# Norm gains moved from the weight rows to the transposed activations, on one core of a two-layer hybrid block

## The chip, the cores and the metric
The kernel runs on one core of a Trainium2 chip. The metric is the device time of one execution in microseconds, median of three runs. TensorE is PE in the profile, VectorE DVE, ScalarE ACT, GpSimd POOL, and SP is the engine whose queue issues the loads.

## The reference, cut to what matters
Batch 1, 256 tokens, width 1024, two layers. Each layer is an FFN, a mixer and a second FFN, each behind an rms norm with a gain vector of 1024 entries:
```
for l in range(DEPTH):
    x = x + 0.5 * swiglu(rms_norm(x, norm_ffn1[l]), ffn1_wi[l], ffn1_wo[l])
    h = rms_norm(x, norm_mix[l])
    (u, q_raw, k_cmp, ..., gate_a, gate_b) = jnp.split(h @ w_in[l], SPLIT_POINTS, axis=-1)
    y_a = s5_branch(u, ...);  y_b = nsa_branch(q_raw, ...) @ nsa_w_up[l]
    x = x + (sigmoid(gate_a) * y_a + sigmoid(gate_b) * y_b) @ w_out[l]
    x = x + 0.5 * swiglu(rms_norm(x, norm_ffn2[l]), ffn2_wi[l], ffn2_wo[l])
# rms_norm(x, g) = x * rsqrt(mean(x*x) + eps) * g
```
The S5 branch is a state space scan over 32 groups. The attention branch has compressed, selected and window keys. D_FF is 2816 and w_in has 3864 columns.

## The kernel before
All weights pass once through a stream of chunks of 128 rows by up to 1024 columns (plan, line 195; most hold two k tiles of 512 columns, those of the third and second mixer products two of 408 and two of 384). A chunk is loaded into a `raw` buffer by the SP queue (`load`, `_dma`) and then split into two numbers of the product's type, `whi` (the rounded value) and `wlo` (the rest), ScalarE writing the one and VectorE the other (`_split0`). A product is three matmuls (`mm3`, lines 350 to 352): hi with hi, hi with lo, lo with hi. There are four buffers each of `raw`, `whi` and `wlo`, and `next` prepares two chunks ahead of the one in use.

The norm's factor 1/rms is a number for each token and is applied after the product, when PSUM is read. Its gain is a number for each row of the weight: where a product follows a norm (the first product of both FFNs and all of w_in), `add` notes which gain vector and which k tile a chunk has, and `_split0` multiplies the rows while it splits them, one k tile at a time (lines 154 to 158): a scaled ACTIVATE on ScalarE and a SCALAR_TENSOR_TENSOR on VectorE for each half. The gains stand as columns in `gcol`, made by a transpose at the start (`gain_cols`, line 290). Chunks without gains (the second product of an FFN, the up-projections, w_out) are split whole by `split` (line 318), as one CAST and one TENSOR_TENSOR.

The activations come token-major in `x`. `transp4` (line 340) transposes 128 tokens by 512 channels on TensorE into one PSUM bank and splits them into `hh` and `hl` with one instruction on each engine. It runs four times at the start and four times in `finish` (line 354), at each of the five boundaries between phases; tile 0's two calls go between the last products of the phase, tile 1's between the first ones of the next. `finish` also leaves a fence: the next chunk's split is queued behind the first subtraction of tile 1. `transp4` serves the merged branches too (line 1293), where there is no norm.

Inside the first FFN of each layer a background generator (`prep`, line 1328) issues the preparation of the S5 branch a little at a time: elementwise work on VectorE and POOL, and transposes on TensorE (line 761). In the mixer another one (`s5_main`, `attn_units`) issues the scan and the attention between the weight products. There line 822 copies a rearranged input on POOL (profiled as line 480), `compress` (line 1020) makes the compressed keys from four chunks that are not split (lines 230 to 233) and then runs its GELU on ScalarE (`hid`, line 1040), and the gates' tanh is line 1264. In the FFN line 451 is the gated product on VectorE, and line 434 its transposes.

The order of instructions on every engine is set by a planner at build time, which goes by program order and by its own prices of instructions; SP's loads keep program order, and `issue_after` puts an instruction behind another on its engine. The functions that the change touches:

Of the kernel before, what the change touches and what calls it, by code (L numbers as in the profile page):

```python
# [7 lines left out]
F32 = mybir.dt.float32  # L8
F32R = mybir.dt.float32r
BF = mybir.dt.bfloat16  # L10
AF = mybir.ActivationFunctionType
ALU = mybir.AluOpType
# [5 lines left out]
L = 2  # L18
# [6 lines left out]
# column offsets of the shape-only constants, packed side by side on 128 partitions  # L25
# [49 lines left out]
class Model:  # L75
# [31 lines left out]
    def add(k, ap, split=True, g=None):  # L107
        """g: (norm, first k tile) whose gains scale the rows"""
        k.chunks.append((ap, split, g))
# [31 lines left out]
    def _split0(k, i):  # L141
        r = k.raw.pop(i)
        if not k.chunks[i][1]:
            k.hl[i] = r
            return
        hi = k.pw.tile([128, 1024], F32R, name="whi", bufs=k.opt['nh'])
        lo = k.pw.tile([128, 1024], F32R, name="wlo", bufs=k.opt['nh'])
        g = k.chunks[i][2]
        if g is None:
            k.split(r, hi, lo)  # L150
        else:
            sh = [n for _, n in k.chunks[i][0].ap[1:]]
            kt, w = sh[0], int(np.prod(sh[1:]))
            for j in range(kt):
                s, c = slice(j * w, (j + 1) * w), k.gcol[:, g[0] * 8 + g[1] + j:g[0] * 8 + g[1] + j + 1]
                k.hi_ins[i] = k.nc.scalar.activation(hi[:, s], r[:, s], AF.Copy, scale=c)  # L156
                k.nc.vector.scalar_tensor_tensor(lo[:, s], r[:, s], c, hi[:, s].bitcast(F32), op0=ALU.mult,  # L157
                                                 op1=ALU.subtract)
        k.hl[i] = (hi, lo)
# [15 lines left out]
    def next(k, la=None):  # L175
        """the next chunk of the stream; prepares later ones as far as buffers allow"""
        i = k.nu
        k.nu += 1
        if i and not k.chunks[i - 1][1]:
            k.held -= 1  # L180
        k.prepare(k.opt['LA'] if la is None else la)
        k.pull()
        return k.hl.pop(i)
# [11 lines left out]
    def plan(k):  # L195
# [13 lines left out]
        def ffn(l, wi, wo, n):  # L209
            for c in range(NFF):  # L210
                for i in range(4):
                    k.add(ap2(wi, l, i * 256, 2, c * 256, DFF, 256), g=(n * 2 + l, i * 2))
                for i in range(2):
                    if c:
                        k.add(ap(wo, l, (c - 1) * 256 + i * 128, 1, 0, D))
            for i in range(2):
                k.add(ap(wo, l, (NFF - 1) * 256 + i * 128, 1, 0, D))

        def cols(l, c0, n=512):
            for i in range(4):  # L220
                k.add(ap(k.a['w_in'], l, i * 256, 2, c0, n), g=(2 + l, i * 2))

        A = k.a
        for l in range(L):
            ffn(l, A['ffn1_wi'], A['ffn1_wo'], 0)
            cols(l, C_U)
            cols(l, C_KC, 384)
            cols(l, C_VS, 408)
            w1 = A['cmp_w1']
            for kv in range(2):  # L230
                for i in range(2):
                    k.add(bass.AP(tensor=w1.tensor, offset=w1.offset + ((l * 2 + kv) * 2048 + i * 1024) * 128,
                                  ap=[[128, 128], [128 * 128, 8], [1, 128]]), split=False)
            for c0 in (C_Q, C_GA, C_GA + 512, C_GB, C_GB + 512):
                cols(l, c0)
            for c in range(4):
                for i in range(2):
                    k.add(ap2(A['ssm_w_glu'], l, i * 256, 2, c * 256, D, 256))
            for c in range(2):
                for i in range(2):  # L240
                    w = A['nsa_w_up']
                    k.add(tuple(bass.AP(tensor=w.tensor, offset=w.offset + (l * 512 + g * 256 + i * 128) * D + c * 512,
                                        ap=[[D, 64], [64 * D, 2], [1, 512]]) for g in range(2)))
            for i in range(8):
                k.add(ap(A['w_out'], l, i * 128, 1, 0, D))
            ffn(l, A['ffn2_wi'], A['ffn2_wo'], 2)

# [6 lines left out]
    def setup(k):  # L254
# [42 lines left out]
        for h in range(2):  # L297
            for t in range(2):
                f = k.transp4(k.x[:, t, h * 512:(h + 1) * 512], t, h)
# [16 lines left out]
    def split(k, src, hi, lo):  # L316
        """hi: src rounded to the product's type, lo: the rest"""
        return k.nc.scalar.copy(hi, src), k.nc.vector.tensor_sub(lo, src, hi.bitcast(F32))  # L318

    def rsqrt(k, ss, n, scale):  # L320
        """(ss*scale + eps)^-0.5 on [P, n]"""
# [13 lines left out]
    def norms(k):  # L335
        """1/rms of both token tiles, behind the weight preparation issued so far"""
        with k.tc.issue_after(k.hi_ins[k.ns - k.opt['SQ']].ins):
            k.rn = [k.rstd(t) for t in range(2)]

    def transp4(k, src, t, half):  # L340
        """four 128x128 transposes of token-major src [128, 512] into hh/hl"""
# [4 lines left out]
        return k.split(b, k.hh[:, s, q], k.hl_[:, s, q]) + (m,)  # L346
# [7 lines left out]
    def finish(k, ys, sc, norm, parts):  # L354
        """x += sc * y and its transposed copy for the next phase. parts: the last products of token tile 0,
        and those of token tile 1 in two portions"""
# [7 lines left out]
        def tr(t):  # L364
            return [k.transp4(k.x[:, t, h * 512:(h + 1) * 512], t, h) for h in range(2)]
# [15 lines left out]
    def gemm(k, stat, nk, cols, order=None, per=2, la=None):  # L381
        """two token tiles against the next weight chunks; returns the two banks.
        order: chunks per turn of a tile where the turns are to be kept"""
# [33 lines left out]
    def ffn(k, hooks, sc, norm, order):  # L417
# [60 lines left out]
        k.finish(y, sc, norm, (lambda: part(0, 0), lambda: wo_mm(last - 1, 1, 1, W), lambda: part(1, 0)))  # L478
# [3 lines left out]
    def mm_cols(k, out, pairs, first, last=True):  # L482
        """sum of lhsT.T @ rhs over pairs, as two column tiles of the array that run side by side"""
# [8 lines left out]
    def s5_load(k, l):  # L492
        """DMAs of the S5 parameters of layer l"""
# [30 lines left out]
    def cmul(k, o, a, b, tmp, cost, M=None, conj=False):  # L524
        """(o0 + i o1) = (a0 +- i a1)(b0 + i b1), products on engine M; tmp(): scratch"""
# [18 lines left out]
    def s5_scalars(k):  # L544
# [31 lines left out]
        # angle to [-pi, pi]  # L576
# [19 lines left out]
        # expm1(a) = 2t/(1-t), cos-1 = -2 sin^2(th/2)  # L596
# [62 lines left out]
        # mag^4 and the unit rotation to the fourth power  # L659
# [11 lines left out]
    def s5_tables(k):  # L671
        """cos, sin of j*phi [128, 16, 64] and the decay of the scan"""
# [46 lines left out]
    def s5_mats(k):  # L719
# [7 lines left out]
        # powers times Bbar, dense: X[(g2 n), p, tau, c], tau = 3 - power  # L727
# [5 lines left out]
        # C transposed, pair-diagonal: CT[(g2 n), p, (g2' c)]  # L733
# [14 lines left out]
        # pair-diagonal copies, then the end-of-chunk input matrices  # L748
# [16 lines left out]
        # lag matrices: rows (tau, g2', c') hold lag 3 - tau  # L765
# [32 lines left out]
        # state-to-output matrices with abar^(s+1)  # L798
# [8 lines left out]
    def s5_main(k, uT):  # L807
        """uT [128 channels, 4, 256] -> yT hi/lo [128 channels, 4, 256]"""
# [56 lines left out]
    def rotate(k, out, x, cs, sn, sl, sign):  # L865
        """out = x * exp(-i*sign*phi*j); for sign < 0 the result is shifted to the next chunk"""
# [40 lines left out]
    def nsa_prep(k, l):  # L907
# [5 lines left out]
        # gains folded into the rotation; 0: q (with the score scale), 1: selection k, 2: window k  # L913
# [23 lines left out]
    def normrope(k, src, nh, cg, sg, out, tabs):  # L937
        """per-head rms norm and rope: src [P, nh, 64] (PSUM) -> out; cg/sg broadcast to [P, nh, 64]"""
# [20 lines left out]
    def kv_evac(k, t, kp, ps):  # L959
        """kp: keys before the norm [128 tokens, 2 branches, 2 heads, 64], ps [tokens, vs | kw | vw | gates]"""  # L960
# [59 lines left out]
    def compress(k, kvT):  # L1020
        """kvT [128 (h d), kv, 256 tokens] -> compressed keys and values"""
# [19 lines left out]
        # keys  # L1041
# [9 lines left out]
    def compress2(k, hid, kb):  # L1051
# [6 lines left out]
        # values  # L1058
# [9 lines left out]
    def u_cmp(k, t):  # L1068
        """compressed branch of query tile t as three stages"""
# [23 lines left out]
        def b():  # L1093
# [5 lines left out]
            # heads come as (r, g), gates as (g, r)  # L1099
# [19 lines left out]
    def u_attn(k, t, r):  # L1119
        """selection and window branches of head r of both groups for query tile t"""  # L1120
# [66 lines left out]
    def attn_units(k):  # L1187
        """the units of both query tiles, three stages deep"""
# [15 lines left out]
    def mix(k):  # L1204
# [107 lines left out]
        k.finish(y, 0.25, True, (lambda: part(0, 0, 3), lambda: part(1, 0, 1), lambda: part(1, 1, 3)))  # L1312
# [6 lines left out]
    def run(k):  # L1319
# [3 lines left out]
        for l in range(L):  # L1323
# [18 lines left out]
            k.ffn({6: h_nsa, 8: lambda: k.nsa_prep(l)}, 0.5, True, k.turns(k.opt['O2'] if l else k.opt['O1']))  # L1342
            k.drain_bg()
            k.mix()
            k.ffn({}, 0.5, l + 1 < L, k.turns(k.opt['O2']))
# [29 lines left out]
```

## Time and profile before

| what | value |
|---|---|
| median of three runs | 1202.55 us (1201.87 to 1202.59) |
| span of the profiled execution | 1202.1 us |
| TensorE busy | 1162.6 us, 97% |
| VectorE busy | 844.5 us, 70% |
| ScalarE busy | 687.7 us, 57% |
| POOL busy | 251.4 us, 21% |
| TensorE's granted clock, mean | 0.995 |

The span runs from the first to the last instruction of one profiled execution; its own time beyond that is not listed. Busy time is the sum over instructions, where matmuls overlap. A row with xN holds N instructions that follow each other, its second number their time together. The bracket behind a row is the engine's idle time just before, and what ended it.

### The profile page before, as it was taken

What the parts mean: (1) busy time and instruction counts of PE and PEld (TensorE: products, weight loads), DVE (VectorE), ACT (ScalarE), POOL (GpSimd) and SP (SyncE); (2) the same over time, 40 slices, a digit from 0 to 9 for tenths busy, and PEclk for the clock granted to TensorE, in tenths of its full rate; (3) what the DMA queues carried; (4) which work ended last, traced back from release to release, by engine and by line L of the source; (5) the groups of instructions that cost most, each with busy time, mean ns of one, the idle gap of its engine ahead of it and who ended that gap; (6) DMA issues with size and microseconds to landing.
All of it is one profiled execution on the core that took longest, in us unless ns stands there. A gap on an engine that the chain in (4) does not pass through costs nothing. (4 is left out here: it accounts for less than half of the span.)

```text
span 1202.1 us, 18057 instructions
## 1 busy us (share of the span) xinstructions
PE 1162.6 (97%) x6326; PEld 947.3 (79%) x6326; DVE 844.5 (70%) x1466; ACT 687.7 (57%) x1228; POOL 251.4 (21%) x320
## 2 busy tenths in 40 slices
PE   7999999989999999999999999999899999999998
PEld 6888777877777888888888887778677778888886
DVE  5797979686865765555667987986967765655554
ACT  6655554738855565555566555555597645655552
POOL 3002654273212000000020053815532110000000
PEclk9999999999999999999999999999899999999999
DMA  7766555453543566656666656455635535666662
GB/s 234 220 182 186 166 156 183 116 158 112 178 126 98 175 210 185 186 182 187 189 183 183 196 160 181 140 155 147 193 89 158 132 117 172 210 179 189 192 183 80
DMA packets 150076, 200.44 MB, mean 167 GB/s; under 512 B 9952, under 2 KB 120832, under 8 KB 149984
## 3 DMA queue, kind: packets, MB, share of 16 engines
q1 hardware_dynamic: 148848, 197.46, 54.0%
q0 software_dynamic: 1136, 1.82, 0.9%
q8 instruction: 50, 0.82, 0.3%
q14 instruction: 42, 0.34, 0.1%
HBM read 198.18 MB, written 1.05 MB: 166 GB/s over the span
## 5 line engine op out<-in xcount | busy, mean ns | idle before, releaser
L157 DVE SCALAR_TENSOR_TENSOR wlo<-raw,gcol,whi 128x512 fp32r<-128x512 f32 (+2 forms) x480 | 363.6, 797 | 104.8 <-ACT whi L156 102.3
L156 ACT ACTIVATE whi<-raw,gcol 128x512 fp32r<-128x512 f32 (+2 forms) x480 | 315.0, 710 | 174.4 <-PE gu L351 78.0
L350 PE MATMUL gu<-whi,hh 128*128 128x512 f32 (+2 forms) x960 | 380.9, 397 | 13.0 <-ACT whi L156 10.6
L352 PE MATMUL gu<-wlo,hh 128*128 128x512 f32 (+2 forms) x960 | 376.1, 395 | 0.0
L351 PE MATMUL gu<-whi,hl 128*128 128x512 f32 (+2 forms) x960 | 375.9, 392 | 0.0
L318 DVE TENSOR_TENSOR wlo<-raw,whi 128x1024 fp32r<-128x1024 f32 x128 | 162.7, 1276 | 109.3 <-ACT whi L318 104.5
L350 PEld LDWEIGHTS gu<-whi,hh 128*128 128x128 f32 x960 | 181.9, 189 | 48.5 <-ACT whi L156 10.8
L318 ACT CAST whi<-raw 128x1024 fp32r<-128x1024 f32 x128 | 134.6, 1054 | 138.2 <-PE gu L351 123.0
L351 PEld LDWEIGHTS gu<-whi,hl 128*128 128x128 f32 x960 | 181.9, 190 | 35.7
L352 PEld LDWEIGHTS gu<-wlo,hh 128*128 128x128 f32 x960 | 181.5, 189 | 35.7 <-DVE wlo L157 0.2
L325 POOL TENSOR_SCALAR rs<-ss 128x1 f32<-128x1 f32 (+3 forms) x22 | 6.6, 301 | 388.7 <-ACT w2k L332 356.0
L351 PE MATMUL yb<-whi,w1k 128*128 128x512 f32 x176 | 71.5, 406 | 0.7 <-DVE w1k L318 0.7
L352 PE MATMUL yb<-wlo,w1k 128*128 128x512 f32 x176 | 69.1, 393 | 0.0
L350 PE MATMUL yb<-whi,w1k 128*128 128x512 f32 x176 | 69.0, 395 | 0.0
L351 PE MATMUL ya<-whi,w1k 128*128 128x512 f32 x176 | 68.8, 391 | 0.0
L352 PE MATMUL ya<-wlo,w1k 128*128 128x512 f32 x176 | 68.7, 390 | 0.0
L350 PE MATMUL ya<-whi,w1k 128*128 128x512 f32 x176 | 68.2, 393 | 0.0
L318 ACT CAST w1k<-tr 128x256 fp32r<-128x256 f32 x88 | 32.4, 369 | 46.3 <-PE tr L434 46.2
L1159 POOL TENSOR_SCALAR w2k<-w2k,sm 128x128 f32<-128x128 f32 (+1 forms) x64 | 33.8, 546 | 109.3 <-ACT w2k L1143 92.4
L451 DVE SCALAR_TENSOR_TENSOR w1k<-gu,rs,w1k 128x256 f32<-128x256 f32 x88 | 41.9, 478 | 20.1 <-ACT w1k L450 20.1
L450 ACT ACTIVATE w1k<-gu,rs 128x256 f32<-128x256 f32 x88 | 40.8, 466 | 21.7 <-PE gu L352 16.8
L318 DVE TENSOR_TENSOR w1k<-tr,w1k 128x256 fp32r<-128x256 f32 x88 | 36.7, 418 | 10.4 <-ACT w1k L318 10.3
(307 smaller groups left out, 1511.2 us busy)
## 6 DMA issues: line engine op xcount, KB each, us to landing
raw<-in_ffn_wi_dram SPq DMA_DIRECT2D x352, 256.0 KB, 3.3
raw<-in_ffn_wo_dram SPq DMA_DIRECT2D x88, 512.0 KB, 3.7
raw<-in_w_in_dram SPq DMA_DIRECT2D x48, 512.0 KB, 4.5
raw<-in_ssm_w_glu_dram SPq DMA_DIRECT2D x32, 256.0 KB, 3.3
raw<-in_w_out_dram SPq DMA_DIRECT2D x16, 512.0 KB, 3.9
raw<-in_cmp_w_dram SPq DMA_DIRECT2D x8, 512.0 KB, 5.5
raw<-in_nsa_w_up_dram SPq DMA_DIRECT2D x16, 256.0 KB, 4.2
raw<-in_w_in_dram SPq DMA_DIRECT2D x8, 408.0 KB, 4.1
```

The lines of the kernel that those rows point to most:

```text
L156: k.hi_ins[i] = k.nc.scalar.activation(hi[:, s], r[:, s], AF.Copy, scale=c)
L157: k.nc.vector.scalar_tensor_tensor(lo[:, s], r[:, s], c, hi[:, s].bitcast(F32), op0=ALU.mult, op1=ALU.subtract)
L318: return k.nc.scalar.copy(hi, src), k.nc.vector.tensor_sub(lo, src, hi.bitcast(F32))
L325: k.nc.gpsimd.tensor_scalar(a, ss, scale, EPS, op0=ALU.mult, op1=ALU.add)
L350: mm(ps, a[0], b[0], start=first, stop=False)
L351: mm(ps, a[1], b[0], start=False, stop=False)
L352: return mm(ps, a[0], b[1], start=False, stop=last)
L450: m = nc.scalar.activation(sg, ps[t][:, :256], AF.Silu, scale=r[t])
L451: nc.vector.scalar_tensor_tensor(a, ps[t][:, 256:], r[t], sg, op0=ALU.mult, op1=ALU.mult)
L1159: G.tensor_scalar(w[:, i], p[:, i], cf[:, j:j + 1], 0.0, op0=ALU.mult, op1=ALU.add)
```

## The change
The gains are no longer multiplied into the weight rows. `add` forgets them, and every chunk that is split goes through `split` in one piece over its whole width (1024 columns, 816 or 768 in the two narrower products of w_in). In their place `transp4` gets the number `g` of the gain vector whose norm follows, and then splits each of its four 128x128 tiles by itself, with that k tile's gain column as the scale on ScalarE and as the factor on VectorE. `finish` hands `g` down: ffn1 gives the mixer's vector (2 + l), the mixer gives ffn2's (4 + l), ffn2 the next layer's ffn1 (l + 1) or None at the end; the first calls have 0. The call on the merged branches has no `g` and stays as it was.
```diff
 def _split0(k, i):
     ...
-    g = k.chunks[i][2]
-    if g is None:
-        k.split(r, hi, lo)
-    else:
-        sh = [n for _, n in k.chunks[i][0].ap[1:]]
-        kt, w = sh[0], int(np.prod(sh[1:]))
-        for j in range(kt):
-            s, c = slice(j * w, (j + 1) * w), k.gcol[:, g[0] * 8 + g[1] + j:g[0] * 8 + g[1] + j + 1]
-            k.hi_ins[i] = k.nc.scalar.activation(hi[:, s], r[:, s], AF.Copy, scale=c)
-            k.nc.vector.scalar_tensor_tensor(lo[:, s], r[:, s], c, hi[:, s].bitcast(F32), op0=ALU.mult,
-                                             op1=ALU.subtract)
+    sh = [n for _, n in k.chunks[i][0].ap[1:]] if not isinstance(k.chunks[i][0], tuple) else [1024]
+    n = int(np.prod(sh))
+    k.hi_ins[i] = k.split(r[:, :n], hi[:, :n], lo[:, :n])[0]
     k.hl[i] = (hi, lo)
...
-def transp4(k, src, t, half):
+def transp4(k, src, t, half, g=None):
     b = k.bank((128, 4, 128))
     for i in range(4):
         m = k.nc.tensor.transpose(b[:, i], src[:, i * 128:(i + 1) * 128], k.id)
     s, q = slice(half * 4, half * 4 + 4), slice(t * 128, (t + 1) * 128)
-    return k.split(b, k.hh[:, s, q], k.hl_[:, s, q]) + (m,)
+    if g is None:
+        return k.split(b, k.hh[:, s, q], k.hl_[:, s, q]) + (m,)
+    for i in range(4):
+        j = half * 4 + i
+        c, hi = k.gcol[:, g * 8 + j:g * 8 + j + 1], k.hh[:, j, q]
+        f = k.nc.scalar.activation(hi, b[:, i], AF.Copy, scale=c)
+        d = k.nc.vector.scalar_tensor_tensor(k.hl_[:, j, q], b[:, i], c, hi.bitcast(F32), op0=ALU.mult,
+                                             op1=ALU.subtract)
+    return f, d, m
```

## Rows read from the trace of the kernel before
**Rows 1.** The page's busy times: us, share of the span, instructions.
```profile
PE 1162.6 (97%) x6326; PEld 947.3 (79%) x6326; DVE 844.5 (70%) x1466; ACT 687.7 (57%) x1228; POOL 251.4 (21%) x320
```
**Rows 2.** Groups by form: busy us, mean ns of one, idle before and releasers.
```profile
L157 DVE SCALAR_TENSOR_TENSOR wlo<-raw,gcol,whi 128x512 fp32r<-128x512 f32 x448 | 342.4, 803 | 97.9 <-ACT whi L156 95.4 <-PE yb L352 1.5
L156 ACT ACTIVATE whi<-raw,gcol 128x512 fp32r<-128x512 f32 x448 | 297.2, 716 | 171.5 <-PE gu L351 75.6 <-PE yb L351 74.4 <-DMA raw<-in_ffn_wi_dram 8.3
...
L318 DVE TENSOR_TENSOR wlo<-raw,whi 128x1024 fp32r<-128x1024 f32 x128 | 162.7, 1276 | 109.3 <-ACT whi L318 104.5 <-PE tr L1169 3.9
L318 ACT CAST whi<-raw 128x1024 fp32r<-128x1024 f32 x128 | 134.6, 1054 | 138.2 <-PE gu L351 123.0 <-DMA raw<-in_ffn_wo_dram 11.5 <-PE yb L351 1.9
```
**Rows 3.** TensorE's waits: us in total, times, longest us.
```profile
PE gu L350 <- ACT whi L156: 10.6, 2, 5.3
...
PE tr L761 <- DVE w1k L318: 2.8, 2, 1.4
PE tr L434 <- DVE w1k L451: 2.6, 2, 1.3
PE gu L350 <- ACT r L1264: 2.5, 2, 1.3
PE ya L488 <- POOL r L480: 2.4, 2, 1.2
...
PE ya L1079 <- DVE qT L318: 1.0, 2, 0.5
PE yb L351 <- DVE w1k L318: 0.7, 2, 0.3
```
**Rows 4.** Timeline, VectorE, first layer's preparation: start us, us, instructions.
```profile
125.48 2.66 DVE L157 SCALAR_TENSOR_TENSOR wlo<-raw,gcol,whi 128x512 fp32r<-128x512 f32 x2
...
128.46 3.01 DVE L157 SCALAR_TENSOR_TENSOR wlo<-raw,gcol,whi 128x512 fp32r<-128x512 f32 x2
...
132.88 0.41 DVE L318 TENSOR_TENSOR w1k<-tr,w1k 128x256 fp32r<-128x256 f32 x1
...
135.79 2.07 DVE L318 TENSOR_TENSOR wlo<-raw,whi 128x1024 fp32r<-128x1024 f32 x1
```
**Rows 5.** Timeline, ScalarE and TensorE, the same stretch.
```profile
131.68 0.36 ACT L318 CAST w1k<-tr 128x256 fp32r<-128x256 f32 x1
...
133.44 0.63 PE L761 MATMUL tr<-id,r 128*128 128x128 f32 x4 [1.41 <-DVE w1k L318]
```
**Rows 6.** Timeline, VectorE, end of the preparation.
```profile
185.90 2.99 DVE L157 SCALAR_TENSOR_TENSOR wlo<-raw,gcol,whi 128x512 fp32r<-128x512 f32 x2
188.81 0.47 DVE L451 SCALAR_TENSOR_TENSOR w1k<-gu,rs,w1k 128x256 f32<-128x256 f32 x1
```
**Rows 7.** Timeline, POOL, end of the preparation.
```profile
186.84 1.49 POOL L530 TENSOR_TENSOR w2k<-s5q,w2k 128x512 f32<-128x512 f32 x1
```
**Rows 8.** Timeline, POOL and VectorE, ahead of the 408-column product.
```profile
233.63 1.87 POOL L480 TENSOR_SCALAR r<-r 32x256 f32<-32x256 f32 x2
...
233.02 2.91 DVE L157 SCALAR_TENSOR_TENSOR wlo<-raw,gcol,whi 128x408 fp32r<-128x408 f32 x3 [0.70 <-ACT whi L156]
```
**Rows 9.** Timeline, ScalarE and SP, ahead of the q product.
```profile
260.05 0.29 ACT L1040 ACTIVATE hid<-ya,pb 128x30 f32<-128x30 f32 x1 [7.84 <-DVE pb L1039]
260.23 2.54 ACT L156 ACTIVATE whi<-raw,gcol 128x512 fp32r<-128x512 f32 x4
...
251.48 23.15 SPq L112 DMA_DIRECT2D raw<-in_w_in_dram  x11
```
**Rows 10.** Groups by form, the subtraction of transp4.
```profile
L318 DVE TENSOR_TENSOR hl<-tr,hh 128x512 fp32r<-128x512 f32 x32 | 21.6, 687 | 16.9 <-ACT hh L318 16.7
```
**Rows 11.** Timeline, ScalarE and TensorE, boundary between the layers.
```profile
607.08 0.58 ACT L318 CAST hh<-tr 128x512 fp32r<-128x512 f32 x1 [0.17 <-PE tr L344]
...
608.62 0.48 PE L350 MATMUL gu<-whi,hh 128*128 128x512 f32 x1
```
**Rows 12.** The page's DMA issues: KB each, median us to landing.
```profile
raw<-in_w_in_dram SPq DMA_DIRECT2D x48, 512.0 KB, 4.5
```

More of the change, by code (lines that the diff above doesn't have):

```diff
@@ L104, in sb, with add @@
         return k.ps.tile(list(shape), dtype, name=tag, tag=tag, bufs=bufs)
-    def add(k, ap, split=True, g=None):
-        k.chunks.append((ap, split, g))
+    def add(k, ap, split=True):
+        k.chunks.append((ap, split))
     def load(k, o, i):
@@ L207, in ap2, with ffn @@
                            ap=[[width, 128], [128 * width, kt], [half, 2], [1, cols]])
-        def ffn(l, wi, wo, n):
+        def ffn(l, wi, wo):
             for c in range(NFF):
                 for i in range(4):
-                    k.add(ap2(wi, l, i * 256, 2, c * 256, DFF, 256), g=(n * 2 + l, i * 2))
+                    k.add(ap2(wi, l, i * 256, 2, c * 256, DFF, 256))
                 for i in range(2):
@@ L220, in cols @@
             for i in range(4):
-                k.add(ap(k.a['w_in'], l, i * 256, 2, c0, n), g=(2 + l, i * 2))
+                k.add(ap(k.a['w_in'], l, i * 256, 2, c0, n))
         A = k.a
         for l in range(L):
-            ffn(l, A['ffn1_wi'], A['ffn1_wo'], 0)
+            ffn(l, A['ffn1_wi'], A['ffn1_wo'])
             cols(l, C_U)
@@ L245, in plan @@
                 k.add(ap(A['w_out'], l, i * 128, 1, 0, D))
-            ffn(l, A['ffn2_wi'], A['ffn2_wo'], 2)
+            ffn(l, A['ffn2_wi'], A['ffn2_wo'])
     def dma_next(k):
@@ L298, in setup @@
             for t in range(2):
-                f = k.transp4(k.x[:, t, h * 512:(h + 1) * 512], t, h)
+                f = k.transp4(k.x[:, t, h * 512:(h + 1) * 512], t, h, 0)
         with k.tc.issue_after(f[2].ins):
@@ L352, in mm3, with finish @@
         return mm(ps, a[0], b[1], start=False, stop=last)
-    def finish(k, ys, sc, norm, parts):
+    def finish(k, ys, sc, g, parts):
+        norm = g is not None
         def up(t):
@@ L364, in tr @@
         def tr(t):
-            return [k.transp4(k.x[:, t, h * 512:(h + 1) * 512], t, h) for h in range(2)]
+            return [k.transp4(k.x[:, t, h * 512:(h + 1) * 512], t, h, g) for h in range(2)]
         parts[0]()
@@ L415, in hstat, with ffn @@
         return k.hh[:, kk, q], k.hl_[:, kk, q]
-    def ffn(k, hooks, sc, norm, order):
+    def ffn(k, hooks, sc, g, order):
         nc = k.nc
@@ L476, in part @@
                     wo_mm(last, t, i, Ws[i], (h,))
-        k.finish(y, sc, norm, (lambda: part(0, 0), lambda: wo_mm(last - 1, 1, 1, W), lambda: part(1, 0)))
+        k.finish(y, sc, g, (lambda: part(0, 0), lambda: wo_mm(last - 1, 1, 1, W), lambda: part(1, 0)))
     def gcopy(k, o, i):
@@ L1201, in attn_units, with mix @@
                     yield cost * (1 if i - d < 5 else 2)
-    def mix(k):
+    def mix(k, g):
         nc = k.nc
@@ L1310, in part @@
                     mm(5 + i, t, Ws[i], (h,))
-        k.finish(y, 0.25, True, (lambda: part(0, 0, 3), lambda: part(1, 0, 1), lambda: part(1, 1, 3)))
+        k.finish(y, 0.25, g, (lambda: part(0, 0, 3), lambda: part(1, 0, 1), lambda: part(1, 1, 3)))
     @staticmethod
@@ L1341, in run @@
             k.bg, k.budget = prep(), k.opt['BG']
-            k.ffn({6: h_nsa, 8: lambda: k.nsa_prep(l)}, 0.5, True, k.turns(k.opt['O2'] if l else k.opt['O1']))
+            k.ffn({6: h_nsa, 8: lambda: k.nsa_prep(l)}, 0.5, 2 + l, k.turns(k.opt['O2'] if l else k.opt['O1']))
             k.drain_bg()
-            k.mix()
-            k.ffn({}, 0.5, l + 1 < L, k.turns(k.opt['O2']))
+            k.mix(4 + l)
+            k.ffn({}, 0.5, l + 1 if l + 1 < L else None, k.turns(k.opt['O2']))
 def hybrid_kernel(tc, out, opt, **a):
```

## The prediction
> **What bounds the kernel now.** I read the page's sums first. TensorE is busy for 1162.6 us of a span of 1202.1 us [rows 1], so 39.5 us of idle time is all that any edit of VectorE and ScalarE work can give back while TensorE's own instruction list stays as it is, and this change leaves it as it is. The groups of instructions come second [rows 2]: they show the price of preparing a weight chunk with gains (two halves on each engine) and without (one whole). The third view is TensorE's waits [rows 3]. The reader is to see that they come in two kinds of place. The first is the preparation stage inside the first FFN of each layer, where TensorE waits for VectorE, at lines 761, 434 and 351 (2.8, 2.6 and 0.7 us in both layers). The second is the mixer: 10.6 us for the first prepared chunk of the q product, 2.4 us for copies on POOL, 2.5 us for the tanh of line 1264. The waits at the start are for loads of x and of the gains, which the change leaves alone, and nothing is listed for the phase boundaries or for the second FFNs. Last I read the timelines at these places, to see what stands ahead of each late instruction in its engine's queue. The profiled execution's span is 1202.1 us, 0.45 us under the median of the runs (1202.55 us); I work on the span and carry the difference over to the median.
>
> **Weight chunks: work removed, by itself worth nothing.** 240 chunks carry gains. One costs 2 x 716 ns on ScalarE and 2 x 803 ns on VectorE by the means of the 512-column halves; a whole 1024-column split costs 1054 and 1276 ns [rows 2]. Halves overlap a little back to back, so I take busy time over count: 297.2 us / 448 = 0.66 us a half and 342.4 / 448 = 0.76 us. A chunk then saves 0.27 us on ScalarE and 0.25 us on VectorE, some 60 us on each engine over the kernel. Where TensorE runs without a wait this is hidden: ScalarE itself sat idle for 75.6 + 74.4 us ahead of these halves until TensorE gave a buffer back [rows 2]. So what counts is what becomes of each listed wait.
>
> **Preparation stage, beside POOL.** Here VectorE is behind, and its halves are slow: pairs take 2.66, 3.01 and 2.99 us, where a whole-chunk split in the same stage takes 2.07 us [rows 4, 6]. POOL's 512-column product beside them takes 1.49 us [rows 7], the time of one half, so the two engines take turns instruction by instruction. One instruction in place of two means one turn of POOL less for each chunk: 2.66 - 2.07 = 0.6 us to 0.9 us saved, and not 0.25. The instructions that TensorE waits for read PSUM and run at 0.41 and 0.47 us there [rows 4, 6]; only their place in the queue is late.
> First wait (line 761, 1.41 us [rows 5]): two pairs are ahead of the `lo` copy at 132.88, so it could come 0.6 + 0.9 = 1.5 us sooner, at 131.4. But it also needs ScalarE's cast, which runs from 131.68 to 132.04 [rows 5]. The copy then ends at 132.04 + 0.41 = 132.45 and not 133.29, and of the 1.41 us some 0.8 go; late next is that cast, queued behind a weight cast that was whole already. Second wait (line 434, 1.3 us): the pair at 185.90 gives 0.9 us, and a pair ahead of it is split by other work and should give about as much, so line 451 comes 1.8 us sooner, and all of the 1.3 us go. Third (line 351, 0.3 us): I take 0.2. Sum 0.8 + 1.3 + 0.2 = 2.3 us a layer, **-4.6 us**. Bounds: all of it is 2.8 + 2.6 + 0.7 = 6.1 us, and the other end is 0, if the small copies end up behind one more whole chunk.
>
> **Mixer, the copies on POOL.** Just ahead of the 408-column product TensorE waits 1.2 us for POOL's copies of line 480 [rows 3]. Two of these take 1.87 us while VectorE works on three 408-column halves in 2.91 us [rows 8]: turns again. A whole of 816 columns is 1276 x 816/1024 = 1.02 us, some 0.4 us more than such a half at 0.6 us (the 512-column half alone, 0.76, by width), and VectorE has one ready whenever a copy asks. Three copies run beside these: 3 x 0.4 = 1.2 us. Against this the first whole starts about 0.3 us later, for the cast is whole too, and lets a copy through. I take **+0.7 us a layer, +1.4**; the bounds are -0.2 (fewer turns to lose) and +1.2 a layer.
> The Trainium skill, SBUF — State Buffer, section "SBUF: two separate sides", calls the pair of ports that VectorE and GpSimd share an exclusive lock held for the whole instruction, for VectorE operations with two SBUF inputs. By that rule longer VectorE instructions cost POOL more for each turn, which speaks against this change; the doubled times of rows 4, 6 and 7 agree with it.
>
> **Mixer, the first chunk of the q product.** TensorE waits 5.3 us a layer for the first half of a chunk whose preparation starts at 260.23, right behind the `hid` activation of 260.05 [rows 9]. No weight split stands on VectorE ahead of that activation, so the wait doesn't shrink from its front. At its end it grows: the product may start after one half (0.66 us) now, and after the whole (1.05 us) then. **+0.4 us a layer, +0.8**; bounds 0 and +1.0 (its `lo` also beside POOL). Queued behind that cast are the second `hid` and the next chunk, which come no later, since two casts are shorter than four halves.
>
> **Mixer, later.** The tanh of line 1264 (1.3 us a layer [rows 3]) stands behind key casts that wait for a VectorE queue with one weight pair ahead of them, and line 1079 (0.5 us a layer) waits for a query copy with one pair ahead. No POOL work runs beside these pairs; each saves 0.2 us. Twice 0.2 us a layer: **-0.8 us**, bounds -3.5 (both waits gone: 2.5 + 1.0) and 0.
>
> **Transposes with gains.** 24 calls (4 at the start, 4 at each of five boundaries) turn one ScalarE cast of 0.58 us [rows 11] and one VectorE subtraction of 0.69 us [rows 10] into four 128-column pieces each. A piece costs at least a quarter of these (0.15 and 0.17 us) and at most what 256 columns from PSUM cost, 0.36 us [rows 5] and 0.41 us [rows 4]; I take the middle, 0.27 us on either engine: 1.1 us a call, +0.5 on ScalarE, +0.4 on VectorE, some +12 and +10 us in all. On the path I put 0. At the boundary at 607 us the cast starts at 607.08 and TensorE takes the tile at 608.62 [rows 11]: four pieces end at 608.2, and the first product needs only the first. The weight casts ahead get shorter besides (2 x 1.05 for 4 x 0.66). Were that cover gone, each boundary would lose up to 0.5 us, 2.5 in all; were TensorE waiting for the first piece, it would gain 0.3 each. The fence now hangs on the last of four subtractions, at most 0.4 us later, ahead of a chunk that is used two turns further on: 0. At the start the gains are transposed ahead of x on TensorE before and after; that the scale has moved to x adds no DMA, and SP's order of loads is unchanged: 0.
>
> **Sum.** -4.6 + 1.4 + 0.8 - 0.8 = -3.2 us: span 1198.9, median **1199.3 us**. From one measurement of this kernel to the next, 0.2% (2.4 us) is about what can be told from no change.
>
> **Rivals.** (a) The relief is taken up by the next wait: the copy of 132.88 and line 451 come sooner, but TensorE then waits for ScalarE or for another VectorE copy, and half of the 4.6 us are left. -2.3 + 1.4 + 0.8 - 0.8 = -0.9: 1201.6 us. For it: VectorE is behind through the whole stage. Against it: at line 434 the cast had long been done and only the queue was late.
> (b) Slower, by turns on the shared port, in the copies of line 480. If each of the four wholes of 816 columns goes ahead of one copy, the copies pay 4 x 1.02 = 4.1 us less what three of them pay now, which is between nothing and a half each (3 x 0.6): 2.3 to 4.1, in the middle 3.2 us a layer, 6.4 in both, straight onto TensorE, which is already waiting there. The same coarser grain halves the gain of the preparation stage. 6.4 + 0.8 - 0.8 - 2.3 = +4.1: 1206.7 us. It decides from a loss of 1.2 us a layer upward. For it: TensorE is late there already. Against it: VectorE's first whole comes late, and half of the copies are through by then. The lock that the Trainium skill states (SBUF — State Buffer, "SBUF: two separate sides") is the rule by which it would come so.
> (c) The planner, which orders the instructions by its own prices, puts the first q chunk ahead of `hid` on ScalarE. Its load is issued at 251.48 and such loads take 4.5 us [rows 9, 12], so it is there at about 256.0; cast by 257.1 instead of 260.9, it saves 3.8 + 0.4 us a layer against the sum: -3.2 - 8.4, 1190.9 us. For it: prices change everywhere. Against it: that the load came late was so for the planner as well.
> (d) The change does what it says in part: the chunks of line 232 are never split, and those of the 384- and 408-column products stay 768 and 816 wide. Neither alters the sum.
>
> **Chances.** Forecast 0.42 (its own range 1197 to 1201), (a) 0.27, (b) 0.16, (c) 0.08, and 0.07 for an order of the planner that I can't see, to either side. The 8-in-10 range takes in (a) and the forecast and reaches towards (b) and (c): 1193.5 to 1205.5. Faster by over 0.2% (below 1200.1): three quarters of the forecast, (c) and half of the last, 0.45; within 0.2%: the rest of the forecast and nearly all of (a), 0.37; slower: (b) and a bit, 0.18.
>
> **What would show it.** Right: VectorE down by about 50 us and ScalarE by about 50; the waits at 761 and 434 at 1.2 us and 0 in both layers together; the wait of line 488 for POOL up from 2.4 to about 3.8, that of the q product from 10.6 to 11.4; none at the boundaries. Wrong: a wait for `hh` or `hl` at a boundary, a new wait for `wlo`, or the q product's wait gone.

## The result and the profile after

The changed kernel is slower. Its median is 1209.09 us (1208.93 to 1211.06, four runs) against 1202.57 us (1201.87 to 1202.72, four runs) for the kernel before. The two medians stand 1.0054 to 1; over the single runs the ratio is put at 1.0061, 95% interval 1.0048 to 1.0073, and the ratios of the experiments below are of that kind. The forecast was 1199.3 us, so the sign was wrong too, and the time lies above the range, which ended at 1205.5.

The page of the changed kernel, busy times and groups (columns as in [rows 1, 2]). Its line 309 is `split`, lines 342 and 343 are the ScalarE and the VectorE piece of `transp4`, and lines 349 to 351 are the three matmuls of `mm3`; line 335 has the transposes of `transp4`, line 435 those of the FFN.
```profile
PE 1164.2 (96%) x6326; PEld 944.8 (78%) x6326; DVE 809.4 (67%) x1298; ACT 637.0 (53%) x1060; POOL 264.0 (22%) x320
...
L309 DVE TENSOR_TENSOR wlo<-raw,whi 128x1024 fp32r<-128x1024 f32 (+2 forms) x368 | 462.7, 1264 | 252.5 <-ACT whi L309 244.8
L309 ACT CAST whi<-raw 128x1024 fp32r<-128x1024 f32 (+2 forms) x368 | 381.4, 1043 | 306.3 <-PE gu L350 183.7
```
The split engines did get lighter: VectorE lost 35.1 us and ScalarE 50.7 us of busy time (844.5 and 687.7 in [rows 1]), against some 50 each that I named. TensorE's instruction count is the same, its busy time rose by 1.6 us and its idle time grew from 39.5 to 42.7 us (span less busy time; in these totals of an engine overlapping instructions count once).

TensorE's waits in the changed kernel (us in total, times, longest):
```profile
PE gu L349 <- ACT whi L309: 11.9, 2, 6.0
PE tr L435 <- DVE w1k L452: 6.6, 7, 1.4
PE tr L335 <- DVE hl L343: 4.4, 5, 1.5
...
PE gu L349 <- ACT hh L342: 2.4, 3, 0.9
PE ya L1137 <- ACT w2k L1144: 2.2, 2, 1.1
...
PE gu L349 <- ACT r L309: 1.3, 2, 0.7
PE gu L349 <- ACT r L1265: 0.7, 2, 0.3
...
PE gu L350 <- DVE hl L343: 0.3, 1, 0.3
```
Beside [rows 3] this says three things. The wait of line 761 and the wait for POOL's copies are gone. The wait of the q product went from 10.6 to 11.9. And there are waits for `hl` and `hh`, which the list of before does not have. They are the sign that the prediction named as "wrong".

The timeline at the boundary between the layers (start us, us, instructions, idle before and what ended it), ScalarE, then VectorE, then TensorE; it is the boundary of [rows 11]:
```profile
609.55 0.37 ACT L342 ACTIVATE hh<-tr,gcol 128x128 fp32r<-128x128 f32 x1 [0.88 <-PE tr L335]
610.34 0.37 ACT L342 ACTIVATE hh<-tr,gcol 128x128 fp32r<-128x128 f32 x1 [0.42 <-DVE hl L343]
611.13 0.63 ACT L342 ACTIVATE hh<-tr,gcol 128x128 fp32r<-128x128 f32 x2 [0.42 <-DVE hl L343]
...
616.95 0.48 ACT L451 ACTIVATE w1k<-gu,rs 128x256 f32<-128x256 f32 x1 [0.97 <-PE gu L351]
617.32 0.36 ACT L342 ACTIVATE hh<-tr,gcol 128x128 fp32r<-128x128 f32 x1
618.24 0.37 ACT L342 ACTIVATE hh<-tr,gcol 128x128 fp32r<-128x128 f32 x1 [0.55 <-DVE hl L343]
621.31 0.47 ACT L451 ACTIVATE w1k<-gu,rs 128x256 f32<-128x256 f32 x1 [2.70 <-PE gu L351]
...
609.95 0.35 DVE L343 SCALAR_TENSOR_TENSOR hl<-tr,gcol,hh 128x128 fp32r<-128x128 f32 x1 [0.89 <-ACT hh L342]
610.74 0.35 DVE L343 SCALAR_TENSOR_TENSOR hl<-tr,gcol,hh 128x128 fp32r<-128x128 f32 x1 [0.43 <-ACT hh L342]
...
621.82 0.48 DVE L452 SCALAR_TENSOR_TENSOR w1k<-gu,rs,w1k 128x256 f32<-128x256 f32 x1 [2.83 <-ACT w1k L451]
...
608.86 0.66 PE L335 MATMUL tr<-id,x 128*128 128x128 f32 x4 [0.46 <-DVE hl L343]
622.36 0.44 PE L435 MATMUL tr<-id,w1k 128*128 128x128 f32 x2 [1.14 <-DVE w1k L452]
```
Read the two engines together. ScalarE's piece starts at 609.55, VectorE's at 609.95, ScalarE's next at 610.34, VectorE's next at 610.74. Each sits idle for the other: a pair of pieces takes 0.79 us, the sum of the two and a gap, and here no two pieces of one tile run side by side. Other work of both queues gets in between the turns of the second tile: its pieces last from 611.39 to 618.99, and ScalarE's last two come at 617.32 and 618.24, behind the next silu (line 451). TensorE waits in several places: for a PSUM bank that the pieces still hold (line 335), and later for the gated product (line 435). That second wait is no full queue on VectorE: line 452 had stood idle for 2.83 us for the silu of the other token tile, which had stood idle for 2.70 us until TensorE itself had finished the product (line 351). TensorE's order had put the end of that product late and nothing behind it to fill the gap.

### The profile page after: what moved, and what is told of

Same layout as the page of the kernel before. It is cut to its first block, busy times and chain, and to the rows that moved or that the text cites. A ratio compares the mean times of both kernels' runs of the same rounds, so it can differ in the third digit from the quotient of the medians.

```text
span 1206.9 us, 17733 instructions
## 1 busy us (share of the span) xinstructions
PE 1164.2 (96%) x6326; PEld 944.8 (78%) x6326; DVE 809.4 (67%) x1298; ACT 637.0 (53%) x1060; POOL 264.0 (22%) x320
## 4 chain that ended last, share of the span: by engine, by line
PE 82%; DVE 6%; POOL 5%; ACT 3%; issue 2%; DMA 1%; SPq 0%; DVEq 0%; ACTq 0%; POOLq 0%
PE gu L349 18%; PE gu L351 17%; PE gu L350 17%; PE yb L350 4%; PE yb L349 4%; PE yb L351 3%; PE ya L351 3%; PE ya L349 3%; PE ya L350 3%; POOL r L481 3%; PE tr L435 2%; PE yb L1181 1%; PE tr L335 1%; ACT whi L309 1%; DVE wlo L309 1%
## 5 line engine op out<-in xcount | busy, mean ns | idle before, releaser
L309 DVE TENSOR_TENSOR wlo<-raw,whi 128x1024 fp32r<-128x1024 f32 (+2 forms) x368 | 462.7, 1264 | 252.5 <-ACT whi L309 244.8
L309 ACT CAST whi<-raw 128x1024 fp32r<-128x1024 f32 (+2 forms) x368 | 381.4, 1043 | 306.3 <-PE gu L350 183.7
L349 PE MATMUL gu<-whi,hh 128*128 128x512 f32 (+2 forms) x960 | 383.0, 399 | 15.0 <-ACT whi L309 11.9
L316 POOL TENSOR_SCALAR rs<-ss 128x1 f32<-128x1 f32 (+3 forms) x22 | 9.5, 432 | 399.3 <-ACT w2k L323 371.1
L342 ACT ACTIVATE hh<-tr,gcol 128x128 fp32r<-128x128 f32 x96 | 32.4, 364 | 29.9 <-PE tr L335 18.1
L343 DVE SCALAR_TENSOR_TENSOR hl<-tr,gcol,hh 128x128 fp32r<-128x128 f32 x96 | 31.2, 347 | 23.5 <-ACT hh L342 23.4
```

Of the source, the lines that this page charges most:

```text
L342: f = k.nc.scalar.activation(hi, b[:, i], AF.Copy, scale=c)
L343: d = k.nc.vector.scalar_tensor_tensor(k.hl_[:, j, q], b[:, i], c, hi.bitcast(F32), op0=ALU.mult, op1=ALU.subtract)
L349: mm(ps, a[0], b[0], start=first, stop=False)
```

## The experiments

All were timed in five rounds, each against runs of the kernel before on the same chip. They ran on three chips: the four from whole chunks alone to the scaled copy on one, pieces read from SBUF on a second, the other three on a third. The kernel before took 1202.17, 1202.07 and 1201.80 us there, so a difference between experiments of two chips is uncertain by some 0.4 us more. A first useful table splits the executions by the start of TensorE's eight transposes of tile 0 at each boundary, and by the start of the last VectorE instruction (1196.38 us in the kernel before, 1202.68 in the changed one). Stage lengths in us, with two experiments that follow:

| stage | before | changed | whole chunks alone | four then four |
|---|---|---|---|---|
| start and FFN 1, layer 1 | 208.08 | 206.36 | 205.58 | 204.75 |
| mixer, layer 1 | 204.60 | 204.07 | 203.20 | 202.86 |
| FFN 2, layer 1 | 188.35 | 192.53 | 188.36 | 188.39 |
| FFN 1, layer 2 | 199.69 | 199.87 | 197.81 | 197.80 |
| mixer, layer 2 | 204.66 | 204.40 | 203.71 | 203.25 |
| FFN 2, layer 2 | 191.00 | 195.45 | 190.99 | 190.99 |

**Whole chunks alone.** The changed kernel with the boundary split of before; the gains are left out of the computation altogether.
```diff
-        if g is None:
+        if True:
             return k.split(b, k.hh[:, s, q], k.hl_[:, s, q]) + (m,)
```


> Only the weight part of the change: chunks are split whole, and the transposed tiles are split by one instruction on each engine as before (the gains of the norms are left out of the result). Theory A (turns): the loss comes from the four pieces of a transposed tile, which ScalarE and VectorE take in turns, each waiting for the other; without them the time is under that of before, 1196 to 1200 us, and TensorE has no wait at the boundaries. Theory B (grain): whole chunks hold up POOL and the small VectorE copies; then this kernel is as slow as the changed one, 1206 to 1210 us. Theory C (work): the pieces cost by their number of instructions, not by their turns; 1196 to 1200 us as in A.


Measured: 1195.26 us, ratio 0.9943 [0.993, 0.9955], a little below the range of A and C. So the coarser grain (B) costs nothing that shows. In the table both FFN 1 stages are shorter than before (2.50 and 1.88 us) and both mixers (1.40 and 0.95); the second FFNs are as long as they were. Its waits:
```profile
PE gu L349 <- ACT whi L309: 11.9, 2, 5.9
...
PE tr L435 <- DVE w1k L452: 2.8, 4, 0.7
PE ya L1137 <- ACT w2k L1144: 2.2, 2, 1.1
PE gu L349 <- ACT r L309: 1.4, 2, 0.7
```
None is for `hh` or `hl`. The changed kernel, which differs from this one by the pieces alone, is longer in every stage: by 0.78, 0.87, 4.17, 2.06, 0.69 and 4.46 us, together 13.0 us.

**Pieces alone.** The halves of before, with their gains on the rows, and the pieces in turns at the boundaries. The pieces take gain vector 0 everywhere, on top of the gains on the rows, so a gain enters twice.
```diff
-        return k.split(b, k.hh[:, s, q], k.hl_[:, s, q]) + (m,)
+        for i in range(4):
+            ...the changed kernel's two instructions for piece i
```


> Only the transposes' part: weights are scaled and split in halves as before, and the transposed tiles go through the four scaled pieces on top (so the gains enter twice). Theories A and C: the boundaries lose what they lose in the changed kernel and the weights give nothing back, 1209 to 1215 us. Theory B: 1202 to 1204 us.


Measured: 1221.2 us, ratio 1.0159 [1.0146, 1.0173]. The pieces cost 19 us here, more than A or C had foreseen. Its waits:
```profile
PE tr L344 <- DVE hl L352: 6.7, 5, 1.8
PE tr L442 <- DVE w1k L459: 6.1, 5, 1.3
...
PE gu L358 <- ACT hh L351: 2.6, 3, 1.1
```
The waits are the changed kernel's, and the one for `hl` is longer.

**Four, then four.** The same eight instructions for each tile as in the changed kernel, in another order.
```diff
-        for i in range(4):
-            ...f = activation of piece i, d = scalar_tensor_tensor of piece i
+        f = [k.nc.scalar.activation(H[i], b[:, i], AF.Copy, scale=C[i]) for i in range(4)][3]
+        d = [k.nc.vector.scalar_tensor_tensor(..., b[:, i], C[i], H[i].bitcast(F32), ...) for i in range(4)][3]
```


> The changed kernel with one edit: the four ScalarE pieces of a tile are issued first and then the four VectorE pieces, so that no piece waits for a turn of the other engine. The instructions and their work are the same. Theory A: most of the loss goes, 1197 to 1201 us. Theory C: it stays, 1206 to 1210 us. Theory B: it stays.


Measured: 1195.06 us, ratio 0.994 [0.9927, 0.9954], below the range that A gave. The number of instructions is unchanged and the slowdown is gone, 14.0 us under the changed kernel, so C falls and A stands. ScalarE and VectorE at the boundary between the layers (timeline):
```profile
601.91 1.14 ACT L341 ACTIVATE hh<-tr,gcol 128x128 fp32r<-128x128 f32 x4 [0.72 <-PE tr L335]
...
603.08 1.12 DVE L342 SCALAR_TENSOR_TENSOR hl<-tr,gcol,hh 128x128 fp32r<-128x128 f32 x4 [1.86 <-ACT hh L341]
```
Four pieces now take 1.14 us on ScalarE, that is 0.28 us each, and VectorE's four follow in 1.12 us. The ScalarE group by form (busy us, mean ns, idle before and its releasers) of the changed kernel, and then of this one:
```profile
L342 ACT ACTIVATE hh<-tr,gcol 128x128 fp32r<-128x128 f32 x96 | 32.4, 364 | 29.9 <-PE tr L335 18.1 <-DVE hl L343 11.8
```
```profile
L341 ACT ACTIVATE hh<-tr,gcol 128x128 fp32r<-128x128 f32 x96 | 26.9, 376 | 20.2 <-PE tr L335 20.2
```
One instruction takes as long as before (364 and 376 ns). What is gone is the 11.8 us for which ScalarE waited for VectorE, and 5.5 us of overlap between neighbours came back. It is the fastest kernel of the study and beats both the kernel before and the changed one.

**Scaled copy.** VectorE multiplies the PSUM tile by the four gain columns into SBUF, and `split` takes that tile whole.
```diff
-        for i in range(4):
-            ...
+        xg = k.sb([128, 4, 128], "w2k", k.opt['n2'])
+        gc = k.gcol[:, g * 8 + half * 4:g * 8 + half * 4 + 4]
+        k.nc.vector.tensor_mul(xg, b, gc[:, :, None].to_broadcast([128, 4, 128]))
+        return k.split(xg, k.hh[:, s, q], k.hl_[:, s, q]) + (m,)
```


> The changed kernel with other instructions for the gains: VectorE multiplies the PSUM tile by the broadcast gain columns into SBUF (one instruction), and that copy is split whole. One VectorE instruction of about 0.7 us more than before for a call, no pieces. Theory A: 1197 to 1202 us, a little more than with four pieces after each other if the later hi costs TensorE at the boundaries. Theory C: 1198 to 1202 us, under the kernel with four and four. Theory B: 1206 to 1210 us.


Measured: 1202.13 us, ratio 1.0001 [0.9993, 1.001], which is just above the range. No pieces, no turns; but one more full pass over the tile stands ahead of the first product, and TensorE waits for `hh`:
```profile
PE gu L346 <- ACT hh L309: 1.2, 2, 0.6
```
That is 1.2 of the 7.1 us by which this kernel is slower than four-then-four. TensorE's busy time is 4.4 us higher (1163.9 against 1159.5); where that comes from is not shown.

What makes the turns was still open: the PSUM tile that both engines read, or the SBUF tile `hh`, which ScalarE writes and VectorE reads.

**An own SBUF tile for each k tile of hh**, pieces in turns as in the changed kernel (the branch without gains becomes four copies and then four subtractions, since there is no common tile to write whole).
```diff
-        k.hh = k.pc.tile([128, 8, SEQ], F32R, name="hh")
+        k.hh = [k.pc.tile([128, SEQ], F32R, name=f"hh{j}") for j in range(8)]
 ...
```


> The changed kernel, pieces in turns, but each k tile of hh has an SBUF tile of its own, so that no two pieces write one tile; they still read one PSUM tile. What makes the turns: (P) the PSUM tile that both engines read: the turns stay, period 0.79 us a piece at the boundary, TensorE waits for hl and w1k as in the changed kernel, 1206 to 1212 us. (H) the SBUF tile hh, written by ScalarE while VectorE reads it: the turns go, pieces 0.37 us apart on ScalarE, 1194 to 1197 us like four-then-four.


Measured: 1208.49 us, ratio 1.0058 [1.0045, 1.0071], the time of the changed kernel. The turns are all there; its timeline on ScalarE, and then its waits:
```profile
611.06 0.37 ACT L345 ACTIVATE hh<-tr,gcol 128x128 fp32r<-128x128 f32 x1 [0.42 <-DVE hl L346]
```
```profile
PE tr L335 <- DVE hl L346: 6.8, 6, 3.4
PE tr L438 <- DVE w1k L455: 6.4, 7, 1.1
...
PE gu L352 <- ACT hh L345: 2.3, 3, 0.8
```
(Of the 6.8 us for `hl`, 3.4 are at the start, where the other runs list the load of x.) So it is not the SBUF tile `hh`.

**Pieces read from SBUF.** Again in turns in program order, but VectorE first copies the four transposes out of PSUM, and both engines read the copy.
```diff
+        c4 = k.sb([128, 4, 128], "w2k", k.opt['n2'])
+        k.nc.vector.tensor_copy(c4, b)
...
-            f = k.nc.scalar.activation(hi, b[:, i], AF.Copy, scale=c)
+            f = k.nc.scalar.activation(hi, c4[:, i], AF.Copy, scale=c)
 ...the same for VectorE's piece
```


> The changed kernel's pieces, in the changed kernel's order (ScalarE piece, VectorE piece, next ScalarE piece), but VectorE first copies the four transposes from PSUM to SBUF in one instruction, and both engines read the SBUF copy. If two engines reading one PSUM tile are what makes the turns (P): ScalarE's pieces follow each other with no wait for hl, and what is left is the cost of the copy, as in the scaled-copy kernel (1202) plus its many small instructions: 1198 to 1205 us. If anything else about the pieces in turn (their number, the order in which they are issued, the tile hh) makes them: 1209 or more, with waits of ScalarE for hl 0.4 us a piece. Against four-then-four (1195), with the same 24 x 4 pieces on each engine, it prices the copy, some 0.4 to 0.7 us on the path at each of 6 stage ends x 4 tiles.


Measured: 1196.98 us, ratio 0.996 [0.9946, 0.9973], a little better than the range. ScalarE's pieces at the same boundary, and their group by form:
```profile
603.53 1.28 ACT L344 ACTIVATE hh<-w2k,gcol 128x128 fp32r<-128x128 f32 x4 [0.88 <-DVE w2k L340]
```
```profile
L344 ACT ACTIVATE hh<-w2k,gcol 128x128 fp32r<-128x128 f32 x96 | 29.9, 390 | 17.7 <-DVE w2k L340 17.7
```
With the order of the code unchanged, no piece waits for `hl` any more. The turns come from two engines reading one PSUM tile: 12 us go although a copy of 0.69 us a tile was added. The traces show it as a wait and not as a slower read: in the changed kernel 32 of ScalarE's 96 pieces stand idle until VectorE has written `hl`, which ScalarE does not read; here and in four-then-four none does.

**Four, then four, with the old halves.** The gains stay on the activations; every chunk that had gains before is cast and subtracted in two halves, without a gain.
```diff
-        k.hi_ins[i] = k.split(r[:, :n], hi[:, :n], lo[:, :n])[0]
+        kt = sh[0] if k.gain[i] else 1
+        for j in range(kt):
+            s = slice(j * n // kt, (j + 1) * n // kt)
+            k.hi_ins[i] = k.split(r[:, s], hi[:, s], lo[:, s])[0]
 ...and transp4 as in four-then-four
```


> Four ScalarE pieces, then four VectorE pieces, with the gains on the transposed activations, and weights cast and subtracted in the old halves (no gain on rows). Against the kernel with in-turn pieces and halves (1221) it prices the turns at the old grain; against four-then-four with whole chunks (1195) it prices the grain alone. If the grain's worth is what whole chunks alone showed (7 us, preparation -4.4 and mixers -2.4): 1200 to 1204. If ScalarE and VectorE work at the halves' grain is what made the in-turn pieces cost 19 instead of 13: 1206 to 1212. First q chunk: its first TensorE wait back from 5.9 to about 5.3 a layer.


Measured: 1198.54 us, ratio 0.9969 [0.9959, 0.9979]; below its ranges. Whole chunks instead of halves are worth 3.5 us (1198.54 to 1195.06), half of the 7 us that "whole chunks alone" showed against before: the rest, 3.3 us against 1201.8 for the kernel before in the same round, is there with halves too. The groups by form show what it goes with: a half without a gain takes 621 ns on ScalarE and 729 on VectorE, where one with a gain took 716 and 803 [rows 2].
```profile
L314 DVE TENSOR_TENSOR wlo<-raw,whi 128x512 fp32r<-128x512 f32 x448 | 308.8, 729 | 98.7 <-ACT whi L314 96.5 <-PE yb L355 1.4 <-PE gu L355 0.4
...
L314 ACT CAST whi<-raw 128x512 fp32r<-128x512 f32 x448 | 253.5, 621 | 174.4 <-PE yb L354 87.7 <-PE gu L354 69.9 <-DMA raw<-in_ffn_wi_dram 5.9
```
At this grain the turns cost 1221.2 - 1198.54 = 22.7 us (with the gains in both places on the one side of this), more than the 14.0 at the whole grain. With the pieces as the only difference it is 19.0 us with halves (pieces alone against the kernel before) and 13.8 with wholes (the changed kernel against whole chunks alone). The wait for the first q chunk is no shorter with halves (TensorE's waits):
```profile
PE gu L353 <- ACT whi L314: 12.5, 2, 6.2
```
But its end is. The first `hid` and the first matmul of the q product, here and then in the changed kernel (timeline, ScalarE and TensorE):
```profile
258.35 0.29 ACT L1045 ACTIVATE hid<-ya,pb 128x30 f32<-128x30 f32 x1 [8.89 <-DVE pb L1044]
259.20 0.79 PE L353 MATMUL gu<-whi,hh 128*128 128x512 f32 x1 [6.23 <-ACT whi L314]
```
```profile
258.49 0.29 ACT L1041 ACTIVATE hid<-ya,pb 128x30 f32<-128x30 f32 x1 [8.19 <-DVE pb L1040]
259.76 0.80 PE L349 MATMUL gu<-whi,hh 128*128 128x512 f32 x1 [5.96 <-ACT whi L309]
```
From `hid` to the product it is 0.85 us with halves and 1.27 with a whole. What grew is the front: from the end of TensorE's work before (the matmul's start less its idle time) to `hid` it is 5.38 us here and 4.69 in the changed kernel.

**The q chunk ahead of the gelu** (rival (c), forced). Four-then-four, with `hid` of the compression put behind the cast of the first q chunk on ScalarE.
```diff
 ...
+            with k.tc.issue_after(k.hi_ins[q0].ins):
-            S.activation(hid[:, kv, :, 0:15], ps[:, 0:2], AF.Gelu_apprx_tanh, bias=pb)
+                S.activation(hid[:, kv, :, 0:15], P[kv][:, 0:2], AF.Gelu_apprx_tanh, bias=pb)
```


> Four-then-four, with the first gelu of the compression (hid) put behind the cast of the first q chunk on ScalarE. The rows of four-then-four: the chunk's load lands some 5.3 us after its issue at 247.1, about 252.4, and the cast starts at 256.14 behind the gelu at 255.95, which waits for TensorE's own products until 255.77. Theory: the gelu's place in the queue is the end of the wait: the q wait of TensorE falls from 5.9 to 2.2 to 3 us a layer, 1187 to 1190 us. Rival: the load lands no earlier than the cast starts now (landing spread up to 9 us): wait 5 to 6 us, 1194 to 1196. Rival: the compression comes late in turn and TensorE waits for it further on: 1193 to 1197 with a new wait for hid, kc or gate.


Measured: 1196.6 us, ratio 0.9956 [0.9943, 0.997], against 0.994 [0.9927, 0.9954] of four-then-four: no gain. Its timeline, ScalarE, VectorE, TensorE:
```profile
250.26 1.05 ACT L309 CAST whi<-raw 128x1024 fp32r<-128x1024 f32 x1 [4.22 <-DMA raw<-in_w_in_dram]
...
253.65 1.73 DVE L879 TENSOR_TENSOR w2k<-r,r 128x504 f32<-128x504 f32 x1
...
256.04 2.27 DVE L309 TENSOR_TENSOR wlo<-raw,whi 128x1024 fp32r<-128x1024 f32 x1
...
251.36 0.50 PE L348 MATMUL gu<-whi,hh 128*128 128x512 f32 x1 [0.52 <-ACT whi L309]
258.36 0.80 PE L350 MATMUL gu<-wlo,hh 128*128 128x512 f32 x1 [5.82 <-DVE wlo L309]
```
The cast came 5.9 us sooner than in four-then-four (256.14 there): it starts as its load lands, which ends its idle time, so the rival of the late load falls. But the third matmul needs `wlo`, whose subtraction stands at 256.04 in VectorE's queue, behind the scan's elementwise work. The 5.9 us wait for `whi` became one of 5.82 us for `wlo`. The time is the one that the last rival expected, but the new wait is in another place than it named.

## Why the prediction was wrong

**The step that failed** is "Transposes with gains", and in it the sentence "On the path I put 0". Its estimate of a single piece was good: 0.27 us, against 1.14 / 4 = 0.28 us on ScalarE and the same on VectorE, where the pieces follow each other. What it took for granted is that they do. `transp4` issues ScalarE's piece and VectorE's piece in turn on one PSUM tile, and there ScalarE's next read is put behind VectorE's last: 0.79 us for each pair. The whole tile of before had one turn: its cast ran 0.58 us and its subtraction 0.69 us [rows 10, 11], about 1.3 us. Now the pairs alone are 4 x 0.79 = 3.2 us if nothing comes between, which is 1.9 us a tile more and past the 0.5 us a boundary that I had as the worst case.

A bank is held the longer for it, so the next transposes wait (4.4 us for `hl`), the products wait (2.4 us for `hh`), and the gated products come late (line 435 waits 6.6 us where four-then-four has 2.9). The excess of line 435 is three waits of 1.1 to 1.4 us, one in each stage that starts an FFN behind a boundary (at 431.68, 622.36 and 1028.77); the two other kernels with turns have them too, and none without turns has. That the late pieces made the planner choose the order behind them is argued and not shown.

These lines and the 0.3 us of line 350 make 13.7 us, 10.8 more than in four-then-four. Other waits are a little shorter, so that the idle time is 9.9 us more (42.7 against 32.8 us); the rest of the 14.6 us between the two spans is TensorE's busy time, 4.7 us higher (1164.2 against 1159.5). Some 1.1 us of this, by my estimate, is the clock behind the q waits. Behind 5.96 us of idle time TensorE goes back to work at 259.76 and 856.22 at a granted clock of 0.50 (1.2 of 2.4 GHz), which lasts until 264.3 and 861.6: 4.5 and 5.4 us at half speed. In four-then-four it is 3.2 and 4.5 us (257.22 to 260.4, 846.37 to 850.9). The other 3.6 us I leave open.

A rule of the Trainium skill says what I passed over, in PSUM — Partial Sum Buffer, section "PSUM bank collisions raise a hardware error": two engines must not access one PSUM bank on the same partitions at once, so the compiler's back end makes instructions of different engines on one bank dependent on each other, reads against reads included, ScalarE against VectorE by name. The trace agrees: 0.42 us of idle time ahead of ScalarE's piece, ended by VectorE's `hl`, and none where the pieces read SBUF. Which step of the build put the wait into this program no run shows.

**Preparation stage, -4.6 us:** right in its sum, wrong in its parts. Whole chunks alone shortened the two FFN 1 stages by 2.50 + 1.88 = 4.4 us. But line 761's wait went whole (I had left 1.2 us), while the transposes of the FFN, said to lose all of their 2.6 us, still wait 2.8 us (four times 0.7 where it was twice 1.3); why was not followed up. Most of it was still there in the changed kernel's FFN 1 of layer 1 (1.7 us); in layer 2 the boundary pieces took it back.

**Copies on POOL, +1.4 us:** the longer copies came as forecast, and their price came to nothing. VectorE's work and POOL's copies ahead of the 408-column product, in the kernel before and then with whole chunks alone (timeline):
```profile
229.81 6.62 POOL L480 TENSOR_SCALAR r<-r 32x256 f32<-32x256 f32 x8 [6.78 <-ACT r L1227]
```
```profile
226.66 7.86 POOL L481 TENSOR_SCALAR r<-r 32x256 f32<-32x256 f32 x8 [6.56 <-ACT r L1228]
...
230.11 5.28 DVE L309 TENSOR_TENSOR wlo<-raw,whi 128x816 fp32r<-128x816 f32 x4 [0.93 <-ACT whi L309]
...
234.99 1.39 PE L489 MATMUL ya<-r,r 128*64 128x64 f32 x40
```
The eight copies took 1.24 us longer, at the bound of 1.2 us that I gave; the last two, beside the weight subtractions alone, took 1.81 us before and 2.66 us with wholes. But TensorE's row of 40 matmuls has no idle time ahead of it: the 408-column products now start at 232.86, and several stand ahead of it where in the kernel before the first came at 238.00, behind it. The order of TensorE's queue changed, and that I had not asked. With it rival (b) falls, although it got the sign: the slowdown is at the boundaries and not here.

**First q chunk, +0.8 us:** 11.9 - 10.6 = 1.3 us measured. The reason I gave, that the product must wait for a whole cast instead of a half, is half of it. In the kernel before `hid` starts at 260.05 [rows 9] and the product at 261.00, 0.95 us later; in the changed kernel it is 1.27, so 0.3 us a layer. The other half is the front, which I took as fixed: from the end of TensorE's work before to `hid` it was 4.34 us and is 4.69. Rival (c) did not happen by itself, and forced it brought nothing.

**Mixer, later, -0.8 us:** larger relief and a price with it. The waits of the tanh and of line 1079 went from 2.5 + 1.0 to 0.6 us, near the bound of -3.5. New ones took most of it: 2.2 us for `w2k` (line 1137) and 1.4 us for `r` of line 309. That is what rival (a) described, in another place. Over both mixers whole chunks alone gave 1.40 + 0.95 = 2.35 us where the three terms of the mixers added up to a loss of 1.4.

So the half of the change that I worked out is worth more than I said (7 us, 1195.26 against 1202.2), and the half that I put at 0 costs 14 us. The difference is what the change lost. What stays open is why the turns cost more with halves (19.0 us) than with wholes (13.8).

## What to carry to other kernels

When an edit cuts one instruction into pieces, follow the pieces of both engines through one buffer, and ask of every pair whether they may run at the same time; an estimate of one piece says nothing about that. Where two engines read one PSUM tile, issue all pieces of the first and then all of the second: the same eight instructions took the kernel from 1209.1 to 1195.1 us. And when a wait is moved, look for the second operand of the same product: here `wlo` was due just as late as `whi`.

## What the runs showed of the hardware that I had not expected

- Two engines in turns over 128-column pieces of one PSUM tile need 0.79 us a pair, while each does its four in 1.12 to 1.14 us alone.
- An additional copy of a 128x512 tile from PSUM to SBUF (0.69 us on VectorE, 24 of them) cost the kernel less than 2 us against four-then-four (1196.98 and 1195.06).
- POOL's eight 32x256 copies took 6.62 us where VectorE subtracted 408-column halves beside the later of them, and 7.86 us where it subtracted 816-column wholes.
